# Four edits to the first phase of a hybrid decoder layer on one core: the pace of the decode sample's scores, the engine that takes the low parts of x, the engine that scales the norms' identity, and the order inside a head's split

## The chip, the cores and the metric

The program runs on one core of a Trainium2 chip. Its engines each take their own instructions in order and meet through semaphores: TensorE (PE, with its weight loads shown apart as PEld), VectorE (DVE), ScalarE (ACT), GpSimd (POOL) and SyncE (SP, which here issues nearly all DMA transfers). The metric is the device time of one execution in microseconds. Lower is better.

## The reference, cut to what matters

One layer of a decoder: RMSNorm, one wide projection to q, k, v, u and vc, attention in three dilations for a prompt of 2048 positions, the same attention for 8 decode samples of 4 tokens against a cache of 2048 positions, a gMLP gate, an output projection, an MLP and a gated per-layer embedding, each behind a norm.

```python
z = rmsnorm(h, norm_g) @ w_in                       # (2048 + 32 tokens) x 1024 -> 2560
q, k, v, u, vc = jnp.split(z, ...)                  # 512 columns each
q, k = rope_partial(q, pos), rope_partial(k, pos)
# decode sample: keys gathered by stride 1, 4 and 16 from cache_k (2048 rows, 8 x 64)
s = jnp.einsum('bthd,btkhd->bthk', q, kg) * (HEAD_DIM ** -0.5)
p, lse = softmax_stats(s)
o = jnp.einsum('bthk,btkhd->bthd', p, vg)           # values gathered from cache_v
# prompt: the same, banded, for dilations 1, 4, 16; then gMLP: u * (W_s layernorm(vc) + b)
h = h + concat(attn, gmlp) @ w_out
h = h + relu(rmsnorm(h) @ w_up)**2 @ w_down
h = h + sigmoid(rmsnorm(h) @ w_gate) * (p_ple @ w_ple)
y = rmsnorm(h)
```

Everything is fp32.

## The kernel before, in words

**Three products for one.** An fp32 product is made of three matmuls on rounded operands: each operand is split into a high part (a rounding cast) and a low part (the operand less its high part), and PE adds high x high, high x low and low x high into the same PSUM bank. So in phase A each matmul triple (L306 to L308 for column tiles `f`, L310 to L312 for token tiles `t`) reads `xh`, `xl`, `wh` and `wl`.

**Phase A** is the wide projection and takes the first 615 us. It goes over x three times: pass r=0 makes q and k, r=1 makes v (`t` tiles) and u (`f` tiles), r=2 makes vc (`t` tiles). Each pass goes over four groups g of 544, 512, 512 and 512 columns (tokens; the first group holds the 32 sample tokens), and each group over 8 slices of 128 input features. `x_split` (L190 to L215) makes one slice's `xh` by a cast on ACT (L202) and its `xl` by a subtraction on DVE or POOL (L203); ten slices are live at a time. `w_split` makes `wh` on ACT (L173) and `wl` on DVE (L174). `qk_evac` takes q and k out of PSUM on DVE (L325, L328) into a ring of three tiles `qk`, which come free when SP's stores to `q_d` (L344) and `kT` (L346) have landed.

**The order around the change** is written by the program itself: every engine gets its instructions in the order in which the Python code issues them, and the code is driven by `tick`, which is called after each slice of a unit of matmuls. A tick runs the delayed stores, at most one step of the evacuations, and `bg[1]` steps of a background list `bg[0]`: the rate adds up, and a step is taken when the sum passes one. On that list stand, one behind the other, `sample_k`, `sample_v` and the prologue of the attention. `to_tok` puts `sample_k` there, once k of the sample tokens is known.

**sample_k** makes the decode sample's scores: after two small products with the new keys (L616, L617) it loads rows of `cache_k` (L607) and the broadcast q (L612), and then 48 times multiplies 128 x 1024 elements on POOL (L634) and reduces the product on DVE (L637), one step for each. Two products may be waiting for their reduction. Three of its loads and the first q stand together just ahead of the first product; the text calls these loads the burst. **sample_v** follows at its own rate, 32 casts on ACT (L727) and low parts alternately on DVE and POOL (L728).

**rstd** makes the reciprocal root of a mean square for a group of tokens, four times in phase A and fourteen times in the last phase: PE sums (L97), ACT copies (L104), POOL raises to the power -1/2 (L105), DVE makes a diagonal matrix from the identity (L111; L114 for the 32 sample tokens), PE multiplies it with ones, which spreads it over all partitions (L118, L121), ACT copies that out (L127, L129).

**split_head** makes the operands of a head for the attention in eight steps: ACT casts q and k (L819, L820), POOL subtracts (L811, L813), and `load_piece` (L798) lets SP fetch a later piece. It runs in the prologue for the first head, still inside pass r=2, and between the units of attention for the others. `perm_piece` (L843, ACT) reorders q for the dilations.

**The end of phase A.** The last group's vc tiles go through a Gelu on ACT (L499, tiles `vg`), a layer norm on DVE (L506 to L517, tile `vn`), the spatial product on PE (L531) and the gate on DVE (L544), and when that list is empty the attention begins with its scores on PE (L947), exponentials on ACT (L968) and turns on PE (L976).

Of the kernel before, what the change touches and what calls it, by code (L numbers as in the profile page):

```python
# [8 lines left out]
F32 = mybir.dt.float32  # L9
F32R = mybir.dt.float32r  # L10
AF = mybir.ActivationFunctionType
ALU = mybir.AluOpType
AX = mybir.AxisListType

P = 128
# [5 lines left out]
NS = DB * DS  # L21
# [26 lines left out]
def build(tc, A, stop=9):  # L48
    nc = tc.nc
    V, S, G, T = nc.vector, nc.scalar, nc.gpsimd, nc.tensor  # L50
# [10 lines left out]
    with stack:  # L61
# [4 lines left out]
        ident = cp.tile([P, P], F32, name="ident")  # L66
# [25 lines left out]
        def rstd(ps, nm, ssum, tt, rt, out, tmp, near=1, far=2, sums=None):  # L92
            i0 = int(tt[0][1] < P)
            n = len(tt)
            p = ps.tile([P, 512], F32, tag="sm", name="rc" + nm, bufs=2)
            for i, (o, m) in enumerate(tt):
                T.matmul(p[:m, i:i + 1], ssum[:, o:o + m], ones[:, 0:1], start=True, stop=True)  # L97
            for _ in range(near):
                yield
            t2 = tmp(0)  # L100
            if i0:
                S.copy(t2[:NS, 0:1], p[:NS, 0:1])
                G.tensor_tensor(rt[:NS, 0:1], t2[:NS, 0:1], half[:NS, 0:1], op=ALU.pow)
            S.copy(t2[:, i0:n], p[:, i0:n])  # L104
            G.tensor_tensor(rt[:, i0:n], t2[:, i0:n], half[:, i0:n], op=ALU.pow)  # L105
            for _ in range(far):
                yield
            w = P * (n - i0)
            dg, ds = tmp(1)
            dgv = dg[:, :w].rearrange("p (a b) -> p a b", b=P)  # L110
            V.tensor_mul(dgv, ident.unsqueeze(1).to_broadcast([P, n - i0, P]),  # L111
                         rt[:, i0:n].unsqueeze(2).to_broadcast([P, n - i0, P]))
            if i0:
                V.tensor_scalar(ds, ident[:NS, :NS], rt[:NS, 0:1], None, op0=ALU.mult)  # L114
            for _ in range(near):
                yield
            p = ps.tile([P, 512], F32, tag="sm", name="rb" + nm, bufs=2)
            T.matmul(p[:, :w], one1, dg[:, :w], start=True, stop=True)  # L118
            if i0:
                p2 = ps.tile([P, 512], F32, tag="sm", name="rs" + nm, bufs=2)  # L120
                T.matmul(p2[:, :NS], one1[:NS, :], ds, start=True, stop=True)  # L121
            for _ in range(near):
                yield
            o0 = tt[i0][0]
            if sums is not None:
                sums.append(p[:, :w])
            S.copy(out[:, o0:o0 + w], p[:, :w])  # L127
            if i0:
                S.copy(out[:, 0:NS], p2[:, :NS])  # L129


        def phase_a(sa, ape, prologue):
# [8 lines left out]
            ktok = kp.tile([P, AW], F32, name="ktok")  # L141
# [50 lines left out]
            def x_split():  # L192
                if x_pos[1] == len(x_items):
                    return
                r, g, k = x_items[x_pos[1]]
                n = GROUPS[g][1]
                x_load(x_pos[1] + 1)
                x_pos[2] = clock[0]
                raw = x_raw.pop((r, g, k))
                h = kp.tile([P, GM], F32R, tag="xh", name=f"xh{r}{g}_{k}", bufs=XB)[:, :n]  # L200
                l = kp.tile([P, GM], F32R, tag="xl", name=f"xl{r}{g}_{k}", bufs=XB)[:, :n]
                S.copy(h, raw)  # L202
                (G if r == 2 or (r == 0 and g == 0) else V).tensor_sub(l, raw, h.bitcast(F32))  # L203
                if r == 0:
                    if k == 0:
                        ss[g] = xw.tile([P, GM], F32, tag="ssum", name=f"ss{g}")[:, :n]
                    sq = xw.tile([P, GM], F32, tag="sq", name=f"sq{g}_{k}")[:, :n]
                    S.activation(sq, raw, AF.Square)
                    if k == 0:
                        V.tensor_scalar(ss[g], sq, 8 * EPS, None, op0=ALU.add)  # L210
                    else:
                        V.tensor_add(ss[g], ss[g], sq)
                X[r, g, k] = (h, l)
                x_pos[1] += 1
# [134 lines left out]
            def to_tok(sf, dst, nm):  # L349
# [6 lines left out]
                if nm == "q":  # L356
                    after(2, lambda: nc.sync.dma_start(qs_d, dst))
                else:
                    bg[0].append(sample_k(sb, ktok[:NS], sT, snew))
                    bg[1] = 0.36  # L360


            sb = {t: ape.tile([P, SEQ], F32, tag=t, name="s" + t) for t in ("kl0", "q10", "kh0", "qd2")}
# [212 lines left out]
            return [sb[t].rearrange("p (h j f) -> p h j f", h=2, j=2)[:, x] for t in names for x in range(2)]  # L576


        def sample_k(sb, ktok, sT, snew):
            qbs = halves(sb, ["kl0"])  # L580
            prods = halves(sb, ["q10", "kh0"])
            kts = halves(sb, ["r0", "r1", "qd2"])
# [37 lines left out]
            for t in range(3):  # L620
                load(t)
            load_q(0)
            yield
            load_q(1)
            for t, (b, jj, d) in enumerate(items):
                if len(prs) == 2:
# [175 lines left out]
        def split_head(x):  # L802
# [3 lines left out]
            q1 = atp[hh].tile([P, SEQ], F32R, tag=f"q1{hh}", name=f"q1_{a}_{hh}")  # L806
            kh = atp[hh].tile([P, SEQ], F32R, tag=f"kh{hh}", name=f"kh_{a}_{hh}")
            head[x] = (q1, kh, kl)
            for j in range(9):
                if j:  # L810
                    G.tensor_sub(timed(q1[ot, c]), q[me].rearrange("p (n r a) -> p n r a", r=16, a=8),  # L811
                                 timed(q1[me, c].bitcast(F32)))
                    G.tensor_sub(kl[:, c], k, kh[:, c].bitcast(F32))  # L813
                if j % 2 == 0 and (j or x == 1):
                    load_piece()
                if j < 8:
                    c = slice(256 * j, 256 * j + 256)
                    k, q = (place(4 * x + j // 2)[y][:, 256 * (j % 2):256 * (j % 2) + 256] for y in range(2))
# [995 lines left out]
```

## Time and profile before

| | |
|---|---|
| median of 3 runs | 2939.37 us (2938.58 to 2942.21) |
| the profiled execution's own time | 2937.39 us |
| its span on the core | 2935.6 us |
| PE busy | 2804.6 us, 96% |
| DVE, ACT, POOL busy | 1566.5, 1277.3, 1228.1 us |
| mean granted TensorE clock | 0.973 of full speed |

The span is the time from the first instruction to the last, and 1.8 us lie around it. In a row of the trace the first numbers are the start and the length in us, then follow the engine, the line of the kernel, the operation, output and inputs and the tile's shape; a bracket at the end says how long the engine had been idle before, and which instruction or transfer released it. Engine times overlap, so a busy sum is no time of the kernel; what counts is where PE stands idle.

### The profile page before, as it was taken

How to read it: one execution, taken by the hardware profiler on the slowest of the kernel's cores; microseconds unless marked ns; L12 is line 12 of the kernel's file. 1: busy time of each engine (PE TensorE's matmuls, PEld its weight loads, DVE VectorE, ACT ScalarE, POOL GpSimd, SP SyncE). 2: the span in 40 equal slices, each digit the busy share in tenths (PEclk: the TensorE clock that was granted, in tenths of full speed). 3: DMA queues.
4: the chain of work that ended last, by engine and by line, in shares of the span. 5: the costliest groups of instructions: out<-in, count | busy, mean ns of one | idle time of the engine just before them, and what ended most of it. 6: DMA issues, size and time to landing. Idle time of an engine off the chain costs nothing.

```text
span 2935.6 us, 42217 instructions
## 1 busy us (share of the span) xinstructions
PE 2804.6 (96%) x15712; PEld 2406.1 (82%) x15712; DVE 1566.5 (53%) x3001; ACT 1277.3 (44%) x2293; POOL 1228.1 (42%) x867
## 2 busy tenths in 40 slices
PE   8998998979899898899999999999999999999998
PEld 8776875669888798799999798888888888888887
DVE  6487447655544457754445544546535356535347
ACT  4122253347778674433334333334433434433342
POOL 2255335545668574533223333334333333433332
PEclk9998999979999999899999999999999999999999
DMA  6458766455765765222222242422233423333232
GB/s 188 142 190 286 244 210 221 142 150 176 229 218 160 242 190 187 76 94 87 87 91 85 77 136 93 169 92 99 82 127 114 145 93 101 101 113 122 94 108 71
DMA packets 218478, 413.34 MB, mean 141 GB/s; under 512 B 19552, under 2 KB 87680, under 8 KB 218272
## 3 DMA queue, kind: packets, MB, share of 16 engines
q1 hardware_dynamic: 215584, 406.45, 42.9%
q10 hardware_dynamic: 2688, 4.20, 0.4%
q8 instruction: 124, 2.03, 0.3%
q14 instruction: 82, 0.67, 0.1%
HBM read 342.61 MB, written 67.96 MB: 140 GB/s over the span
## 4 chain that ended last, share of the span: by engine, by line
PE 57%; DVE 2%; ACT 1%; issue 1%; POOL 0%; POOLq 0%; ACTq 0%
PE u L1445 8%; PE u L1443 8%; PE u L1444 8%; PE d L1443 8%; PE d L1444 8%; PE d L1445 8%; PE g L1445 2%; PE g L1444 2%; PE g L1443 2%; DVE ss L1367 1%; PE b L1445 1%; PE b L1443 1%; PE b L1444 1%; DVE zf L1407 0%; ACT sq L1362 0%
## 5 line engine op out<-in xcount | busy, mean ns | idle before, releaser
L1288 POOL TENSOR_TENSOR w<-wraw,w 128x1024 fp32r<-128x1024 f32 x228 | 558.9, 2454 | 993.8 <-ACT w L1287 955.6
L1287 ACT CAST w<-wraw 128x1024 fp32r<-128x1024 f32 x304 | 316.4, 1045 | 368.6 <-PE d L1444 259.8
L1443 PE MATMUL d<-ring,w 128*128 128x512 f32 (+2 forms) x1312 | 458.2, 349 | 0.9 <-ACT ring L1479 0.9
L1493 DVE TENSOR_TENSOR acc<-acc,d 128x512 f32<-128x512 f32 (+2 forms) x640 | 361.0, 578 | 180.9 <-PE d L1445 180.0
L1443 PE MATMUL u<-zh,w 128*128 128x512 f32 (+1 forms) x1280 | 454.0, 355 | 3.0 <-ACT sq L1362 1.8
L1444 PE MATMUL d<-ring,w 128*128 128x512 f32 (+2 forms) x1312 | 455.3, 347 | 0.3 <-DVE ring L1480 0.3
L1445 PE MATMUL d<-ring,w 128*128 128x512 f32 (+2 forms) x1312 | 455.3, 347 | 0.0
L1445 PE MATMUL u<-zh,w 128*128 128x512 f32 (+1 forms) x1280 | 452.1, 353 | 0.0
L1444 PE MATMUL u<-zl,w 128*128 128x512 f32 (+1 forms) x1280 | 449.8, 351 | 2.2 <-POOL zl L1411 1.3
L1480 DVE TENSOR_TENSOR ring<-r,ring 128x512 fp32r<-128x512 f32 (+1 forms) x160 | 112.4, 703 | 514.8 <-ACT ring L1479 514.8
L1443 PEld LDWEIGHTS d<-ring,w 128*128 128x128 f32 x1312 | 248.0, 189 | 32.8 <-ACT ring L1479 1.1
L1445 PEld LDWEIGHTS d<-ring,w 128*128 128x128 f32 x1312 | 247.3, 188 | 33.1
L1444 PEld LDWEIGHTS d<-ring,w 128*128 128x128 f32 x1312 | 247.7, 189 | 31.2 <-DVE ring L1480 0.5
L1444 PEld LDWEIGHTS u<-zl,w 128*128 128x128 f32 x1280 | 242.3, 189 | 37.4 <-issue 1.7
L1443 PEld LDWEIGHTS u<-zh,w 128*128 128x128 f32 x1280 | 241.6, 189 | 37.1 <-ACT sq L1362 2.0
L1445 PEld LDWEIGHTS u<-zh,w 128*128 128x128 f32 x1280 | 241.8, 189 | 32.7
L1477 ACT ACTIVATE r<-u 128x512 f32<-128x512 f32 (+1 forms) x160 | 82.6, 516 | 290.2 <-PE u L1445 290.2
L1136 POOL TENSOR_TENSOR fl<-fr,fh 128x512 fp32r<-128x512 f32 (+1 forms) x120 | 128.5, 1076 | 134.4 <-ACT fh L1135 112.6
L306 PE MATMUL f<-xh,wh 128*128 128x512 f32 (+1 forms) x480 | 174.8, 364 | 8.5 <-ACT wh L173 5.6
L307 PE MATMUL f<-xl,wh 128*128 128x512 f32 (+1 forms) x480 | 172.3, 359 | 7.5 <-DVE xl L203 7.5
L958 DVE CUSTOM_DVE_ANT_0 sm<-s,mask 128x256 f32<-128x256 f32 (+1 forms) x384 | 122.3, 363 | 103.4 <-ACT pe L968 34.1
L308 PE MATMUL f<-xh,wl 128*128 128x512 f32 (+1 forms) x480 | 172.7, 360 | 0.4 <-DVE wl L174 0.4
(279 smaller groups left out, 5708.5 us busy)
## 6 DMA issues: line engine op xcount, KB each, us to landing
wraw<-w_up SPq DMA_DIRECT2D x128, 512.0 KB
wraw<-w_down SPq DMA_DIRECT2D x128, 512.0 KB
xr<-xT SPq DMA_DIRECT2D x72, 256.0 KB
sr<-cache_v SPq DMA_DIRECT2D x32, 512.0 KB
wraw<-w_gate SPq DMA_DIRECT2D x32, 512.0 KB
fr<-g_d SPq DMA_DIRECT2D x24, 512.0 KB
wr<-w_in SPq DMA_DIRECT2D x40, 256.0 KB
o_d<-stg SPq DMA_DIRECT2D x32, 264.0 KB
```

What stands on the lines that cost most here:

```text
L306: T.matmul(p, wh[:, k, ws], h[:, o:o + w], start=st, stop=False)
L307: T.matmul(p, wh[:, k, ws], l[:, o:o + w], start=False, stop=False)
L308: T.matmul(p, wl[:, k, ws], h[:, o:o + w], start=False, stop=sp)
L958: V.tensor_tensor_reduce(sm[:, c], sp[:, c], mask[:, 256 * d + (256 - P * nk if d < 2 else 0):256 * d + (256 if d < 2 else P)], scale=1.0, ...
L1136: G.tensor_sub(l, raw, h.bitcast(F32))
L1287: S.copy(w[:, 0], raw)
L1288: (V if t % 4 == 3 else G).tensor_sub(w[:, 1], raw, w[:, 0].bitcast(F32))
L1443: T.matmul(p, wh, zh, start=(x == 0), stop=False)
L1444: T.matmul(p, wh, zl, start=False, stop=False)
L1445: T.matmul(p, wl, zh, start=False, stop=(x == n - 1))
L1480: V.tensor_sub(hl[:, c], r, hh[:, c].bitcast(F32))
L1493: V.tensor_add(acc[g][:, d, c], acc[g][:, d, c], p)
```

## The change

Four edits. `to_tok` hands `sample_k` the rate setter `pace` and starts it at 0.8 steps per tick, and `sample_k` sets 0.38 when it has issued its first loads; before, the rate was 0.36 throughout. `x_split` gives POOL the low parts of pass r=1 as well, so DVE keeps those of r=0, groups 1 to 3, alone. `rstd` makes its diagonal on ACT, with one copy scaled by a per-partition number for each 128 columns, in place of one multiplication on DVE. `split_head` takes ten steps, and the loads stand at odd steps ahead of POOL's subtractions.

```diff
@@ rstd
-            V.tensor_mul(dgv, ident.unsqueeze(1).to_broadcast([P, n - i0, P]),
-                         rt[:, i0:n].unsqueeze(2).to_broadcast([P, n - i0, P]))
+            for a in range(n - i0):
+                S.activation(dgv[:, a, :], ident, AF.Copy, scale=rt[:, i0 + a:i0 + a + 1])
             if i0:
-                V.tensor_scalar(ds, ident[:NS, :NS], rt[:NS, 0:1], None, op0=ALU.mult)
+                S.activation(ds, ident[:NS, :NS], AF.Copy, scale=rt[:NS, 0:1])
@@ x_split
-                (G if r == 2 or (r == 0 and g == 0) else V).tensor_sub(l, raw, h.bitcast(F32))
+                (G if r or g == 0 else V).tensor_sub(l, raw, h.bitcast(F32))
@@ to_tok
-                    bg[0].append(sample_k(sb, ktok[:NS], sT, snew))
-                    bg[1] = 0.36
+                    bg[0].append(sample_k(sb, ktok[:NS], sT, snew, pace))
+                    bg[1] = 0.8
@@ sample_k
-        def sample_k(sb, ktok, sT, snew):
+        def sample_k(sb, ktok, sT, snew, pace):
...
             load_q(0)
-            yield
+            yield from pace(0.38)
             load_q(1)
@@ split_head
-            for j in range(9):
-                if j:
+            for j in range(10):
+                if j % 2 and (j > 1 or x == 1):
+                    load_piece()
+                if 0 < j < 9:
                     G.tensor_sub(timed(q1[ot, c]), q[me].rearrange("p (n r a) -> p n r a", r=16, a=8),
                                  timed(q1[me, c].bitcast(F32)))
                     G.tensor_sub(kl[:, c], k, kh[:, c].bitcast(F32))
-                if j % 2 == 0 and (j or x == 1):
-                    load_piece()
```

What this does to the engines' orders is shown at three places. First, SP in pass r=0, from the load of the sample's q (`skl`, L591) on; `sr` and `sqd` are the tiles for rows of cache_k, `xr` slices of x, `qk` tiles of q and k. Before, right behind that load:

```order
L188 DMA xr_4_1004<-xT 128x512
L344 DMA q_d<-qk_0_2_994 128x512
L344 DMA q_d<-qk_0_3_1002 128x512
L188 DMA xr_5_1033<-xT 128x512
L188 DMA xr_6_1076<-xT 128x512
L188 DMA xr_7_1096<-xT 128x512
L188 DMA xr_0_1113<-xT 128x512
L607 DMA sr_113<-cache_k 128x512
L607 DMA sr_113<-cache_k 128x1024
L607 DMA sr_114<-cache_k 128x1024
L612 DMA skl_109<-qs_d 128x1024
L344 DMA q_d<-qk_0_0_948 128x512
```

After, right behind the same load:

```order
L607 DMA sr_113<-cache_k 128x512
L607 DMA sr_113<-cache_k 128x1024
L607 DMA sr_114<-cache_k 128x1024
L612 DMA skl_109<-qs_d 128x1024 x2
L607 DMA sqd_112<-cache_k 128x1024
L188 DMA xr_4_1022<-xT 128x512
L344 DMA q_d<-qk_0_2_1010 128x512
L344 DMA q_d<-qk_0_3_1020 128x512
L607 DMA sqd_112<-cache_k 128x1024
L188 DMA xr_5_1054<-xT 128x512
```

The burst has moved ahead of four slices of x and two stores, and away from the store of `qk_0_0`, the tile that it stood right in front of.

Second, the border of passes r=0 and r=1. On DVE before, from the first low part of pass r=1 (`xl_0`, 544 columns) on:

```order
L203 TENSOR_TENSOR xl_0_1711<-xr_0_1476,xh_0_1710 128x544
L325 SCALAR_TENSOR_TENSOR qk_0_2_1714<-f_0_2_0_1603,rstd_b 128x512
L174 SCALAR_TENSOR_TENSOR wl_1688<-wr_1_510,gains,wh_1687 128x512
L325 SCALAR_TENSOR_TENSOR qk_0_3_1726<-f_0_3_0_1604,rstd_b 128x512
L637 TENSOR_REDUCE sT_107<-sq_110 128x16
L174 SCALAR_TENSOR_TENSOR wl_1688<-wr_2_1689,gains,wh_1687 128x512
L203 TENSOR_TENSOR xl_1_1751<-xr_1_1493,xh_1_1750 128x544
L174 SCALAR_TENSOR_TENSOR wl_1688<-wr_3_1716,gains,wh_1687 128x512
L637 TENSOR_REDUCE sT_107<-sq_110 128x16
L203 TENSOR_TENSOR xl_2_1785<-xr_2_1510,xh_2_1784 128x544
```

And on POOL after, from the same low part on:

```order
L203 TENSOR_TENSOR xl_0_1745<-xr_0_1504,xh_0_1744 128x544
L634 TENSOR_TENSOR sq_110<-sr_114,skl_109 128x1024
L203 TENSOR_TENSOR xl_1_1785<-xr_1_1521,xh_1_1784 128x544
L634 TENSOR_TENSOR skh_111<-sr_113,skl_109 128x1024
L203 TENSOR_TENSOR xl_2_1820<-xr_2_1541,xh_2_1819 128x544
L203 TENSOR_TENSOR xl_3_1837<-xr_3_1549,xh_3_1836 128x544
L634 TENSOR_TENSOR skh_111<-sqd_112,skl_109 128x1024
L203 TENSOR_TENSOR xl_4_1854<-xr_4_1762,xh_4_1853 128x544
L203 TENSOR_TENSOR xl_5_1873<-xr_5_1795,xh_5_1872 128x544
L203 TENSOR_TENSOR xl_6_1887<-xr_6_1842,xh_6_1886 128x544
L634 TENSOR_TENSOR sq_110<-sqd_112,skl_109 128x1024
L203 TENSOR_TENSOR xl_7_1908<-xr_7_1860,xh_7_1907 128x544
```

The low parts have left the queue of evacuations, weight parts and reductions on DVE, and stand among four of sample_k's products on POOL.

Third, ACT at the end of phase A, the last two Gelus of vc (`vg_256`, `vg_384`) and the store of the last gate. Before:

```order
L819 CAST q_0_0_4719<-stage_4591 64x2x16x8
L820 CAST kh_0_4720<-stage_4591 128x256
L843 CAST qd_4916<-q_0_0_4719 128x512
L499 ACTIVATE vg_256_4925<-t_4_256_4803,rstd_t 128x512
L843 CAST qd_4916<-q_0_0_4719 128x512 x2
L499 ACTIVATE vg_384_4948<-t_4_384_4877,rstd_t 128x512
L546 DMA g_d<-gt_384_4981 128x4x128
```

After:

```order
L843 CAST qd_4742<-q_0_0_4399 128x512 x2
L499 ACTIVATE vg_0_4854<-t_4_0_4750,rstd_t 128x512
L499 ACTIVATE vg_128_4856<-t_4_128_4751,rstd_t 128x512
L499 ACTIVATE vg_256_4939<-t_4_256_4846,rstd_t 128x512
L499 ACTIVATE vg_384_4960<-t_4_384_4898,rstd_t 128x512
L546 DMA g_d<-gt_384_4993 128x4x128
```

The first head's casts and its three reorderings have all moved ahead of the last group's Gelus, and nothing stands between the last two of these.

## Rows read from the trace of the kernel before

**Rows 1.** Windows by stage: bounds and length, busy per engine, PEclk, DMA share, GB/s.

```profile
0.00:615.00 615.00, 569.44 (x2784) 444.06 (x2784) 390.96 (x559) 202.91 (x387) 261.05 (x149) 0.96 0.61 198
615.00:655.00 40.00, 24.76 (x119) 21.57 (x119) 15.48 (x64) 24.18 (x49) 13.28 (x24) 0.56 0.65 183
1200.00:2935.60 1735.60, 1712.81 (x9261) 1483.45 (x9259) 861.66 (x1282) 670.21 (x1036) 607.08 (x276) 0.99 0.31 103
```

**Rows 2.** Timeline of PE, 119 to 136 us.

```profile
125.71 0.50 PE L307 MATMUL f<-xl,wh 128*128 128x512 f32 x1 [2.58 <-DVE xl L203]
...
131.25 0.51 PE L307 MATMUL f<-xl,wh 128*128 128x512 f32 x1 [3.87 <-DVE xl L203]
```

**Rows 3.** Timeline of DVE, 108 to 134 us.

```profile
123.36 0.69 DVE L328 TENSOR_TENSOR qk<-f,rstd_b 128x512 f32<-128x512 f32 x1 [7.98 <-DMA q_d<-qk]
125.58 2.86 DVE L212 TENSOR_TENSOR ss<-ss,sq 128x512 f32<-128x512 f32 x1
128.37 2.83 DVE L203 TENSOR_TENSOR xl<-xr,xh 128x512 fp32r<-128x512 f32 x1
```

**Rows 4.** Windows around the two stalls of phase A, and a stretch between them.

```profile
130.00:140.00 10.00, 8.75 (x28) 7.28 (x29) 7.12 (x8) 0.16 (x1) 4.76 (x4) 0.66 0.72 237
220.00:245.00 25.00, 15.36 (x44) 8.47 (x45) 23.35 (x24) 6.35 (x10) 10.56 (x4) 0.73 0.77 253
140.00:200.00 60.00, 59.00 (x256) 47.02 (x255) 50.96 (x48) 17.46 (x30) 39.12 (x17) 1.00 0.70 246
```

**Rows 5.** Groups by line on PE, 219.9 to 240.8 us: busy, mean ns, idle before.

```profile
L312 PE MATMUL t<-wl,xh 128*32 128x512 f32 (+1 forms) x11 | 5.5, 504 | 2.1 <-DVE wl L174 2.1
L311 PE MATMUL t<-wh,xl 128*32 128x512 f32 (+1 forms) x11 | 5.5, 502 | 7.6 <-DVE xl L203 7.6
```

**Rows 6.** Groups by line and shape, whole span: busy, mean ns, idle before.

```profile
L634 POOL TENSOR_TENSOR skh<-sr,skl 128x1024 f32<-128x1024 f32 x16 | 40.0, 2505 | 68.3 <-DMA q_d<-qk 41.1 <-DVE sT L637 14.6 <-DMA wr<-w_in 6.7
L203 POOL TENSOR_TENSOR xl<-xr,xh 128x512 fp32r<-128x512 f32 x24 | 35.5, 1486 | 27.0 <-ACT xh L202 27.0
L203 DVE TENSOR_TENSOR xl<-xr,xh 128x512 fp32r<-128x512 f32 x48 | 40.5, 848 | 39.3 <-ACT xh L202 39.0
L203 POOL TENSOR_TENSOR xl<-xr,xh 128x544 fp32r<-128x544 f32 x16 | 26.0, 1631 | 18.8 <-ACT xh L202 18.4 <-DMA xr<-xT 0.4
```

**Rows 7.** Timeline of DVE: the first low part of pass r=1.

```profile
205.28 2.55 DVE L203 TENSOR_TENSOR xl<-xr,xh 128x544 fp32r<-128x544 f32 x1
```

**Rows 8.** Timeline of PE: the first matmul that reads it.

```profile
218.38 0.40 PE L311 MATMUL t<-wh,xl 128*32 128x512 f32 x1
```

**Rows 9.** Timeline of PE, end of phase A and first scores.

```profile
614.75 0.39 PE L312 MATMUL t<-wl,xh 128*128 128x512 f32 x1
621.71 1.97 PE L531 MATMUL sp<-wsT,vn 128*64 128x128 f32 x16 [6.57 <-DVE vn L517]
...
627.28 0.48 PE L947 MATMUL s<-kh,qd 128*128 128x128 f32 x1
```

**Rows 10.** Timeline of ACT, 600 to 641 us.

```profile
617.09 0.68 ACT L499 ACTIVATE vg<-t,rstd_t 128x512 f32<-128x512 f32 x1
...
619.57 0.69 ACT L499 ACTIVATE vg<-t,rstd_t 128x512 f32<-128x512 f32 x1
...
636.33 1.28 ACT L968 ACT_TABLE_LOAD   x1
637.62 1.28 ACT L968 ACTIVATE pe<-sm,stg 128x128 f32<-128x128 f32 x4
```

**Rows 11.** Timeline of PE, the two waits for a norm's diagonal.

```profile
1191.26 2.04 PE L118 MATMUL rb<-dg,one 128*128 128x512 f32 x2 [7.47 <-DVE dgs L114]
...
2864.31 0.70 PE L118 MATMUL rb<-dg,one 128*128 128x256 f32 x2 [1.25 <-DVE dg L111]
```

**Rows 12.** Timeline of DVE, then of ACT, at 1183 to 1193 us.

```profile
1186.00 5.12 DVE L111 TENSOR_TENSOR dg<-ident,rt 128x512 f32<-128x512 f32 x1
...
1186.00 0.63 ACT L1362 ACTIVATE sq<-acc 128x512 f32<-128x512 f32 x1 [0.76 <-DVE ss L1367]
```

## What the change does to the time: the prediction

> **What bounds the kernel now.** I read the windows by stage first, because the share of busy time is an average. From 1200 us on PE is busy 1712.81 of 1735.60 us at 0.99 of the clock, so nothing that the other engines do there can give back more than a few us. Phase A has 45.6 us of PE idle in 615 (615.00 less 569.44), and the 40 us in which it passes into attention have 15.2 us of idle at 0.56 of the clock [rows 1]. So I went to PE's timeline in phase A for its longest waits, then to the timelines of the engines they name, and to the groups by line for the prices.
>
> Two places stand out. At 125 and 131 us PE waits 2.58 and 3.87 us for `xl` from DVE [rows 2]. DVE is not slow there: it had stood 7.98 us before an evacuation (L328) whose `qk` tile was still being stored to `q_d`, and when it got going, its two-input operations, 0.69 us otherwise, took up to 2.86 us [rows 3]. In program order that store stands right behind the burst of `cache_k` loads (front, first place). At 220 to 241 us, the border of passes r=0 and r=1, PE waits 7.6 us for `xl` and 2.1 us for `wl`, both from DVE [rows 5], which is busy 23.35 of the 25 us [rows 4].
>
> **The change part by part.** The sum is made against the profiled execution's own 2937.39 us; the median shown lies 1.98 us above it, and I add that at the end.
>
> *A, the burst.* The loads move ahead of four slices of x and two stores. The store of `qk_0_0` then no longer queues behind them, and the first product comes in group 1. At stake are 6.45 us of waits [rows 2] and what the clock lost after them: from 130 to 140 us it was granted at 0.66 (between its levels of 1.2 and 2.4 GHz) with PE busy 8.75 us [rows 4], which is 8.75 x 0.34 = 3.0 us. What it will look like, the stretch from 140 to 200 us tells: products run there already (POOL busy 39.12 of 60 us), the same operations of pass r=0 are on DVE, and PE idles 1.00 us [rows 4]. I take -6.5: the waits less 1 us, and a third of the clock's loss. Bounds: -9.4 (all of it) and -2 (the tile is waited for elsewhere in the group).
>
> *B, the border.* The eight low parts of group 0 leave DVE. On POOL each takes 1.63 us and stands among four products of 2.5 us (front, second place; the prices [rows 6]): 8 x 1.63 + 4 x 2.5 = 23.0 us. The first was possible at 205.28 [rows 7], a product may be running (2.5 us), so the last is ready at about 230.8. PE reads the first at 218.38 [rows 8] and goes through a slice in six matmuls of 59.00 / 256 = 0.230 us [rows 4], so it wants the last at 218.4 + 7 x 1.38 = 228.0: 2.8 us late in place of 9.7. DVE, rid of 1.2 to 2.9 us pieces, is then the later one with its `wl`, some 1 to 2 us more. I take -5 and let the clock's loss stand. Bounds: -13.8 (all 9.7 us, and 15.36 x 0.27 = 4.1 us of clock [rows 4]) and +2.5 (one more product ahead of the last low part).
>
> *C, the rest of pass r=1.* POOL's program from the first low part of group 0 to the last product holds 22 products, 8 low parts of 544 and 8 of 512 columns: 22 x 2.5 + 8 x 1.63 + 8 x 1.49 = 80 us. Its products also wait for DVE's reductions, 14.6 us in the 16 of one form [rows 6], 0.9 each, so 20 us: 100 us. PE takes 5 + 4 token tiles of 24 matmuls and as much as 4.25 + 4 column tiles of them in the two groups, 414 x 0.230 = 95 us, and the low parts have a head start of 218.4 - 205.3 = 13.1 us [rows 7, 8]. So POOL falls about 5 us behind and eats less than half of the head start. I take +2 for a slice that meets a product, bounds 0 and +6.
>
> The Trainium skill speaks against this edit: GPSIMD Engine Reference, section 4.1, sends two-input elementwise work to VectorE, since GpSimd is about two times slower at it. This trace agrees nearly, 1486 against 848 ns for 128 x 512 [rows 6], a ratio of 1.75 with DVE's contended pieces in its mean. By the page's two, the eight low parts of group 1 would take 8 x 1.70 in place of 8 x 1.49 us, and POOL would be 7 us behind and not 5, which leaves the term as it is.
>
> *D, sample_v and the first head's split move earlier.* They follow sample_k, which ends about one group sooner, so their POOL and ACT work and their transfers lie in other places of passes r=1 and r=2, and `load_piece` stands ahead of the subtractions. The work is the same and PE covers most of it; I take 0, bounds -3 and +6 (two waits as long as those of [rows 2], less the clock).
>
> One side effect is in ACT's order: the sample's exponentials now fall between the Gelus of u, so two more activation tables are loaded (8 against 6). A load is 1.28 us [rows 10]. ACT is busy 202.91 of 615 us [rows 1] and no matmul soon after reads these Gelus, so I take 0, at most +2.6. The Trainium skill, ScalarE: Activation LUTs, section What ACT_TABLE_LOAD costs, gives about 2.7 us with the drain for each; the row here is half of that, and by the page the bound would be +5.4.
>
> *E, the end of phase A.* The last matmul of vc starts at 614.75, but its Gelu at 619.57, because ACT works off the first head's casts and reorderings in between [rows 9, 10]. After, nothing stands there. From the end of the earlier Gelu (617.77) to its spatial product (621.71) the layer norm takes 3.94 us. So: last matmul done 615.15, Gelu done about 615.9, spatial product 619.8, and after its 1.97 us [rows 9] the scores at 621.8 in place of 627.28. The gate, its store and the first exponential at 637.62 [rows 10] follow by the same amount. I take -5.5; bounds -6.5 and -3 (the layer norms of the last two tiles on DVE one behind the other).
>
> *F, the norms.* At 1191.26 PE has waited 7.47 us for the diagonal [rows 11]; DVE had it under way from 1186.00 for 5.12 us [rows 12]. ACT is free at 1186.63 [rows 12]. Four activations of 128 x 128 take 1.28 us there [rows 10], the small one some 0.2, so PE can go at about 1188.2: -3. Of the wait of 1.25 us at 2864.31 [rows 11] I take 1 off. Where DVE had been fast (the first group's norm, the very last one) four small operations are longer than one, by 0.4 each as I assume from the 1.28: +0.8 together. The other norms are made while PE has matmuls to do. Sum -3, bounds -5 and +1 (a cast of the MLP's weights, queued behind the copies on ACT, comes late).
>
> Sum: -6.5 - 5 + 2 + 0 - 5.5 - 3 = -18. 2937.39 - 18 = 2919.4, and with 1.98 **2921 us**.
>
> **The rivals.** *First, the waits only move.* Another `qk` store holds DVE instead, since all stores still share one queue with the cache loads, and at the border `wl` is late by as much as `xl` was. Then A and B are 0, and 2937.39 - 6.5 + 1.98 = 2933. For it: at 123.36 DVE waits for a DMA, not for POOL, so the transfer could be slow by itself [rows 3]. Against it: the stretch from 140 to 200 us, where loads and stores share the queue and PE idles 1 us [rows 4].
>
> *Second, POOL becomes the bound of pass r=1, and the kernel slower.* A low part waits behind products, a product behind its reduction on DVE, and that behind evacuations which wait for PE. With 80 us of work in 95 + 13 us, PE is reached when a product waits over 28 / 22 = 1.3 us on average; the row has 0.9 [rows 6]. At 2 us POOL is 80 + 44 - 108 = 16 us late, the clock falls as it did at 220 us and costs some 4 more, and B's 5 are gone: 25 on top of 2921 is 2946.
>
> *Third, the earlier prologue collides in pass r=2.* The first head's pieces stand in SP's queue ahead of slices of x and wait for POOL, whose subtractions now meet low parts of the same pass. Three waits like the two of [rows 2], with their clock, are 12 us: 2933. Nothing in the trace rules it out, but the end of phase A gains from the same shift, and that is counted.
>
> **How the numbers follow.** The forecast has 0.62, with its own range of 2908 to 2932 from the bounds of A, B and E; the first rival 0.18, the second 0.10, the third 0.10. A difference under 0.2%, 5.9 us, is what a measurement of this kernel can hardly tell from none, so faster means below 2933.5 and slower above 2945.2. The forecast lies below but for 0.01; of the first and third rival a little over half does; the second is slower by half and more. Faster 0.62 + 0.15 = 0.77, slower 0.08, the rest 0.15 the same. The range of 2906 to 2938 reaches over the first and the third rival and leaves out the second and the ends.
>
> **What would show it right or wrong.** A: no wait for `xl` over 1 us at 115 to 135 us, and the first product below 100 us. B: at the border waits of some 4 us in sum, named POOL `xl` or DVE `wl`. C: no wait for POOL's `xl` over 3 us later in pass r=1. E: scores begin 5 to 6 us nearer to the last vc matmul, the two last Gelus one behind the other. F: the wait before L118 near 1188 us on the old scale is about 4.5 us and names ACT. The prediction is wrong if POOL's `xl` in pass r=1 holds PE for over 15 us in sum, or if pass r=2 shows waits that were not there.

## The result and the profile after

The changed kernel takes 2914.84 us in the median of 4 runs (2914.68 to 2915.15) against 2940.79 us for the kernel before (2938.58 to 2944.29, 4 runs): a ratio of 0.9911, interval 0.9894 to 0.9928, or 26 us. The profiled spans are 2913.3 and 2935.6 us, 22.3 us apart; this is the difference that the stages below add up to. The kernel before varies by several us between executions, which the medians take in and one profile does not.

The windows by stage, as in [rows 1], with bounds moved to the same places of the program (phase A now ends near 603 us):

```profile
0.00:605.00 605.00, 564.30 (x2784) 440.71 (x2784) 365.31 (x527) 214.45 (x411) 300.58 (x184) 0.97 0.63 203
605.00:650.00 45.00, 34.31 (x195) 31.12 (x196) 19.27 (x80) 29.17 (x62) 19.80 (x29) 0.62 0.69 197
1190.00:2913.30 1723.30, 1702.55 (x9220) 1474.20 (x9220) 831.57 (x1256) 679.68 (x1075) 601.66 (x273) 1.00 0.31 103
```

PE's idle time in phase A is 40.7 us where it was 45.6 (1.5 of the 40.7 lie behind the last matmul, which the window before does not have), with the same 2784 matmuls; the rest of the gain there is PE's busy time, 564.3 us against 569.4, at 0.97 of the clock in place of 0.96. Around the two places of [rows 4], 130 to 140 us and 25 us at the border of the passes:

```profile
130.00:140.00 10.00, 10.00 (x43) 7.78 (x42) 4.46 (x6) 3.39 (x8) 10.00 (x6) 1.00 0.99 382
210.00:235.00 25.00, 23.62 (x102) 16.72 (x101) 18.82 (x18) 7.83 (x12) 23.15 (x11) 1.00 0.97 320
```

Both run at the full clock, and PE is idle 1.4 us in the second, where it was idle 9.6. PE's timeline shows the waits that are new, changed or left at the places of the prediction, to be read beside [rows 2], [rows 5] and [rows 9]:

```profile
173.03 0.50 PE L307 MATMUL f<-xl,wh 128*128 128x512 f32 x1 [2.35 <-DVE xl L203]
...
213.58 0.40 PE L311 MATMUL t<-wh,xl 128*32 128x512 f32 x1
...
223.51 0.42 PE L312 MATMUL t<-wl,xh 128*32 128x512 f32 x1 [1.22 <-DVE wl L174]
...
224.72 0.42 PE L311 MATMUL t<-wh,xl 128*32 128x512 f32 x1
...
248.89 0.59 PE L306 MATMUL f<-xh,wh 128*128 128x272 f32 x1 [4.67 <-ACT vo L423]
...
458.71 1.05 PE L739 MATMUL so<-sel,skh 64*128 64x4 f32 x8 [3.38 <-DVE skh L734]
...
603.09 0.39 PE L312 MATMUL t<-wl,xh 128*128 128x512 f32 x1
605.88 1.09 PE L531 MATMUL sp<-wsT,vn 128*64 128x128 f32 x16 [2.40 <-DVE vn L517]
609.61 1.97 PE L531 MATMUL sp<-wsT,vn 128*64 128x128 f32 x16 [2.64 <-DVE vn L517]
611.51 0.48 PE L947 MATMUL s<-kh,qd 128*128 128x128 f32 x1
```

The waits of 2.58 and 3.87 us are gone, one in the next group has grown from 1.00 to 2.35 us, the border has 1.22 us left, and the one for `vo` (a v tile, taken out of PSUM by ACT) is 4.67 us where it was 2.00. At 213.58 and 224.72 us stand the first and the last reading of a low part in the border's first pair of token tiles. From the last vc matmul to the scores it is 8.4 us where it was 12.5.

Where POOL stands at the border, by its timeline (the answer to [rows 7]):

```profile
195.13 1.82 POOL L203 TENSOR_TENSOR xl<-xr,xh 128x544 fp32r<-128x544 f32 x1
196.92 2.84 POOL L634 TENSOR_TENSOR sq<-sr,skl 128x1024 f32<-128x1024 f32 x1
199.72 1.82 POOL L203 TENSOR_TENSOR xl<-xr,xh 128x544 fp32r<-128x544 f32 x1
...
209.92 1.37 POOL L203 TENSOR_TENSOR xl<-xr,xh 128x544 fp32r<-128x544 f32 x1 [3.63 <-ACT xh L202]
...
222.86 1.81 POOL L203 TENSOR_TENSOR xl<-xr,xh 128x544 fp32r<-128x544 f32 x1
```

The first norm of the last phase on ACT, and the wait on PE that goes with it, as in [rows 12] and [rows 11]:

```profile
1170.17 1.26 ACT L112 ACTIVATE dg<-ident,rt 128x128 f32<-128x128 f32 x4
1171.34 0.30 ACT L114 ACTIVATE dgs<-ident,rt 32x32 f32<-32x32 f32 x1
...
1171.49 2.08 PE L118 MATMUL rb<-dg,one 128*128 128x512 f32 x2 [3.89 <-ACT dg L112]
```

Setting the two timelines of PE side by side at the same instruction gives the stages. The columns are the time of that instruction in the two profiles and how the gap grew since the line above; the instructions are the sums of the norms (L97) of groups 1 to 3, the first matmul of v, the first of u, the last of vc, the first scores, and two spreadings of a norm (L118) in the last phase.

```text
                     before    after     gap    grown by
sums, group 1         79.38    80.69    +1.31    +1.31
sums, group 2        133.27   126.81    -6.46    -7.77
sums, group 3        183.03   178.22    -4.81    +1.65
first of v           218.15   213.35    -4.80    +0.01
first of u           261.11   242.93   -18.18   -13.38
last of vc           614.75   603.09   -11.66    +6.52
first scores         627.28   611.51   -15.77    -4.11
first norm, last ph. 1191.26  1171.49  -19.77    -4.00
a later norm         1661.80  1640.78  -21.02    -1.25
end of the span      2935.60  2913.30  -22.30    -1.28
```

(The gap between the first of u and the last of vc is compared at its ends only, since sample_v's matmuls have moved in between. The first line holds nothing of the edits that these runs can tell: `xl_alone`, which leaves that stretch as it was, is 1.85 us late there.)

### The profile page after: what moved, and what is told of

Its sections match the earlier page's. It is cut to its first block, busy times and chain, and to the rows that moved or that the text cites. A ratio compares the mean times of both kernels' runs of the same rounds, so it can differ in the third digit from the quotient of the medians.

```text
span 2913.3 us, 42298 instructions
## 1 busy us (share of the span) xinstructions
PE 2798.0 (96%) x15712; PEld 2399.5 (82%) x15712; DVE 1515.2 (52%) x2947; ACT 1299.9 (45%) x2363; POOL 1265.0 (43%) x899
## 4 chain that ended last, share of the span: by engine, by line
PE 57%; DVE 2%; ACT 1%; issue 0%; POOL 0%; POOLq 0%; ACTq 0%; DVEq 0%
PE u L1445 8%; PE u L1443 8%; PE u L1444 8%; PE d L1443 8%; PE d L1444 8%; PE d L1445 8%; PE g L1445 2%; PE g L1444 2%; PE g L1443 2%; DVE ss L1367 1%; PE b L1443 1%; PE b L1445 1%; PE b L1444 1%; DVE zf L1407 0%; ACT sq L1362 0%
```

## The experiments

Times are medians, set against the kernel before, timed beside them on the same chip. The changed kernel was not timed again beside them, and the medians of the kernel before differ by up to 2.8 us between these groups of runs (2937.96 to 2940.79); so a difference to the changed kernel under some 3 us is not resolved.

**The four edits one by one.** `pace_alone` is the kernel before with the hunks of the diff in `to_tok` and `sample_k`:

```diff
-                    bg[1] = 0.36
+                    bg[1] = 0.8
...
-            yield
+            yield from pace(0.38)
```

> The kernel before with the new pace alone (0.8 up to the first product, 0.38 from there). My theory: this edit carries A and E by itself. The waits of 2.58 and 3.87 us at 125 to 131 us go, with their clock (-7 to -8 us to the third group's sums, as in the changed kernel), and the last Gelus of vc stand one behind the other (-4 us between the last vc matmul and the scores). The border of passes r=0 and r=1 keeps its waits of about 9.7 us, since the low parts are still on DVE. Time -9 to -14 us against before. Rival: the loss at 125 us only went because the low parts are off DVE later and the border had room; then the pace alone moves the products into DVE's busiest stretch, new waits appear there, and the time is within 5 us of before.

Measured: 2925.10 against 2939.67 us, ratio 0.9945 (0.9933 to 0.9958). The places at 125 us and at the end of phase A came as my theory had it (the gap is -7.5 us at the sums of group 2, and -4.1 us from the last vc matmul to the scores). But 3.3 us come back in group 3, another 3.1 us behind it (38.2 us from the sums of group 3 to the first of v in place of 35.1, PE without idle time, at 0.91 of the clock in place of 1.00), and the border did not keep its waits:

```profile
225.37 0.41 PE L311 MATMUL t<-wh,xl 128*32 128x512 f32 x1 [0.93 <-DVE xl L203]
231.79 0.42 PE L312 MATMUL t<-wl,xh 128*32 128x512 f32 x1 [2.34 <-DVE wl L174]
```

With a third of 0.43 us between them, and the low parts still on VectorE, PE waits 3.7 us there in place of 9.7, and the stretch from the first of v to the first of u is 32.3 us where it was 43.0. So VectorE is not too full for the border; something else had made it late.

`xl_alone`:

```diff
-                (G if r == 2 or (r == 0 and g == 0) else V).tensor_sub(l, raw, h.bitcast(F32))
+                (G if r or g == 0 else V).tensor_sub(l, raw, h.bitcast(F32))
```

> The kernel before with the low parts of pass r=1 on GpSimd alone. My theory: the border loses its waits (-13 us there with the clock, as in the changed kernel) and later waits in pass r=1 take some back; the stall at 125 us stays. Time -8 to -13 us. Rival: without the earlier products GpSimd has 27 products left at the border in place of 22 and falls behind, low parts come late in groups 1 and 2, and the time is -5 to +5 us.

Measured: 2932.37 us, ratio 0.9971 (0.9960 to 0.9983), -7.3 us. The border is 34.2 us long, 8.7 less, and 4.7 us of waits for `wl` are left on PE; no wait names a low part on GpSimd in pass r=1. That is a little less than my theory had, for it had put all 13 us of the border down to this edit; the rival is out.

`diag_alone` (the hunk in `rstd`):

> The kernel before with the norms' diagonal on ScalarE alone. My theory: the wait before the first norm of the last phase falls from 7.5 to about 3.9 us, two short waits late in the program change by a few tenths, and the time is -3 to -5 us. Rival: the last phase as a whole gains (the changed kernel is 2.5 us shorter from that norm to the end), because VectorE is rid of nine to fourteen slow operations there; then -6 us or more.

Measured: 2934.51 us, ratio 0.9979 (0.9970 to 0.9989), -5.2 us, just over the theory's end. The wait at the first norm is 3.89 us, as it should be, but the sums of group 3 come 2.7 us later, of which 1.2 are still there at the scores. That the norms of phase A do this is not shown: 1.5 of the 2.7 us stand already at the sums of group 1, where `xl_alone`, with the old diagonal, is late too. The rival, a gain in the whole last phase, is not borne out: from the first norm to the end it is 1742.0 us, and 1741.6 to 1742.7 us in the other single edits with the old diagonal.

`split_alone` (the hunk in `split_head`):

> The kernel before with the new order inside a head's split alone. My theory: the loads move past subtractions in a stretch in which TensorE is covered; -2 to +1 us. Rival: the earlier loads are what lets the first head's casts finish before the last Gelus, and this edit carries the gain at the end of phase A: -4 us or more.

Measured: 2934.53 us, ratio 0.9982 (0.9973 to 0.9991), -5.1 us by the medians and -1.5 by the profiled spans (2934.1 against 2935.6). Neither theory is borne out. From the last vc matmul to the scores it takes 10.1 us in place of 12.5, so a part of the rival's gain is there; but the last vc matmul comes 3.7 us later, and the scores start 1.3 us later than before. No stage of the profile shows a gain of 4 us, and why the medians do stays open.

**One number in place of the edits.** In the kernel before, VectorE had waited 7.98 us for the store of a q tile [rows 3], and the same kind of wait stands in its timeline at the border:

```profile
215.13 0.69 DVE L325 SCALAR_TENSOR_TENSOR qk<-f,rstd_b 128x512 f32<-128x512 f32 x1 [6.04 <-DMA q_d<-qk]
```

These stores are asked for 12 ticks after the tile is made, and SyncE takes its issues in order, so each stands behind loads which wait for free tiles. `store_early` is the kernel before with

```diff
-                    after(12 if g and m < 2 else 2, lambda: nc.sync.dma_start(q_d[m, :, c0 + s0 - NS:c0 + n - NS], o_[:, s0:]))
+                    after(2, lambda: nc.sync.dma_start(q_d[m, :, c0 + s0 - NS:c0 + n - NS], o_[:, s0:]))
```

> The kernel before with one number changed: the stores of the first two q tiles of groups 1 to 3 are asked for 2 ticks after the tile is made, in place of 12, so on SyncE they stand ahead of the burst and of the loads behind it. Theory: both waits of phase A, the one at 125 us and the one at the border of passes r=0 and r=1, begin with VectorE waiting for a q tile whose store stands late in SyncE's queue (7.98 us at 115 us, 6.04 us at 209 us). Then this number alone takes most of both away: -8 to -18 us, with neither the pace nor the low parts moved. Rival for the border: VectorE is simply too full there (23.4 of 25 us busy), so the border keeps over 6 us of waits for xl and only the first place gains: -4 to -9 us. Rival for both: the stores are slow as transfers, the wait stays: within 3 us of before.

Measured: 2919.75 against 2937.96 us, ratio 0.9938 (0.9924 to 0.9952), -18.2 us from a single number. SyncE's timeline has the stores, and VectorE's has the only wait for a q tile that is left between 100 and 240 us:

```profile
94.65 0.93 SPq L344 DMA_DIRECT2D q_d<-qk  x2
96.78 1.45 SPq L344 DMA_DIRECT2D q_d<-qk  x2
...
151.15 0.69 DVE L325 SCALAR_TENSOR_TENSOR qk<-f,rstd_b 128x512 f32<-128x512 f32 x1 [0.36 <-DMA q_d<-qk]
```

and PE's groups by line from 209 to 244 us show the border's waits:

```profile
L311 PE MATMUL t<-wh,xl 128*128 128x512 f32 (+1 forms) x40 | 16.4, 411 | 2.6 <-DVE xl L203 2.6
L312 PE MATMUL t<-wl,xh 128*128 128x512 f32 (+1 forms) x40 | 16.4, 410 | 2.1 <-DVE wl L174 2.1
```

The first store is issued at 94.65 us; before, it stood behind the burst until 113.99:

```profile
112.10 1.37 SPq L607 DMA_DIRECT2D sr<-cache_k  x3
113.52 0.43 SPq L612 DMA_DIRECT2D skl<-qs_d  x1
113.99 0.43 SPq L344 DMA_DIRECT2D q_d<-qk  x1
```

The place at 125 us is gone (-7.5 us at the sums of group 2) and the border keeps 4.7 of 9.7 us (-8.2 us by its length of 34.8). So the late store alone made the first wait, and about half of the second; the rival for both is out, and that for the border (over 6 us of waits for `xl`) too. What was late about it is less its issue than its landing. VectorE began to stand at 115.38, when the store had been issued, and was let go at 123.36, 9.4 us after the issue (8.3 us in `xl_alone`, which keeps the burst in its place); the store at 96.49 had let VectorE go after 2.9 us. In the changed kernel the same store is issued hardly sooner, and VectorE takes the tile at 119.92 without a wait:

```profile
111.26 1.45 SPq L607 DMA_DIRECT2D sr<-cache_k  x1
113.00 0.33 SPq L188 DMA_DIRECT2D xr<-xT  x1
113.38 0.42 SPq L344 DMA_DIRECT2D q_d<-qk  x1
...
119.92 0.68 DVE L328 TENSOR_TENSOR qk<-f,rstd_b 128x512 f32<-128x512 f32 x1
```

One load of `cache_k` is issued in the 2.2 us ahead of it there, in place of three and one of q. VectorE also gets to the tile 4.5 us later than before, having a reduction and a lengthened addition to do, which covers a part.

**What the low parts' move is worth beyond the border.** `pool_g0` is the changed kernel with

```diff
-                (G if r or g == 0 else V).tensor_sub(l, raw, h.bitcast(F32))
+                (G if r == 2 or g == 0 else V).tensor_sub(l, raw, h.bitcast(F32))
```

> The changed kernel, but of pass r=1 only group 0 has its low parts on GpSimd; groups 1 to 3 are back on VectorE. Theory: all that the move to GpSimd earns lies at the border, and the rest of it is neutral, since in the changed kernel no wait in pass r=1 names a low part: +-2 us against the changed kernel, -24 us against before. Rival (term C of the prediction): the low parts of groups 1 to 3 on GpSimd cost 2 us or more through the products and through sample_v, and the time is 2 to 6 us below the changed kernel.

Measured: 2915.54 against 2937.96 us, ratio 0.9921 (0.9908 to 0.9934), within a microsecond of the changed kernel by the medians, 3.5 us by the two differences to the kernel before. The 24 low parts of groups 1 to 3 cost and earn nothing on GpSimd that these runs resolve; the rival, a time below the changed kernel's, is out. The wait for `vo` is there too, 3.93 us, so it does not come from them.

**The changed kernel without one edit.** `no_pace` has the old rate, `no_diag` the old diagonal.

> The changed kernel without the pace: low parts, diagonal and split as changed, the rate 0.36 throughout. Theory: the pace and the low parts each take away the border's wait by themselves, so their gains overlap; what the pace adds on top of the other three is the place at 125 us (-7 us, of which 3 come back in group 3) and the end of phase A (-4 us). So this one is 7 to 11 us slower than the changed kernel, -14 to -18 us against before. Rival: the gains add up, and without the pace 14 us are missing: -9 to -11 us against before.

> The changed kernel with the diagonal back on VectorE. Theory (term F, -3 in the prediction): the first norm of the last phase gives 3.5 us, the short ones a little, and phase A loses 1 to 2 us at its first norm, so without the edit the kernel is 2 to 5 us slower than the changed one, 2917 to 2920. Rival: with the q stores early the edit brought next to nothing in the median, because what the norm gives the earlier stages take back; then the time is within 1.5 us of the changed kernel.

Measured: `no_pace` 2922.17 against 2937.96 us, ratio 0.9941 (0.9929 to 0.9954), 7 us above the changed kernel, as the theory of overlapping gains has it, and the rival is out. Its profile is not as the theory has it: the border takes 36.4 us in place of 29.6, with 4.7 us of waits for `wl`, and 5.7 of these 6.8 us come back between the first of u and the last of vc. `no_diag` 2921.94 against 2938.80 us, ratio 0.9944 (0.9930 to 0.9957), 7 us above it as well, more than the theory's 5, and the rival is out. By the profiles 2.7 us of these stand at the scores (2.1 already at the sums of group 3; what makes them is not shown) and 3.6 at the first norm of the last phase, where PE waits 7.32 us again.

**Towards a faster version.** After the change the one wait over 1 us in groups 1 to 3 of pass r=0 is that at 173 us. `g3_pool` moves eight more low parts, `changed_store` has the early stores in the changed kernel, `g3_and_store` both, and `store_and_diag` is the kernel before with the early stores and the new diagonal only.

```diff
-                (G if r or g == 0 else V).tensor_sub(l, raw, h.bitcast(F32))
+                (G if r or g in (0, 3) else V).tensor_sub(l, raw, h.bitcast(F32))
```

> The changed kernel with the low parts of pass r=0, group 3 on GpSimd as well. Theory: of the waits in the changed kernel's pass r=0 only one of 2.35 us for VectorE's xl is left, at 173 us, where VectorE's two-input operations are stretched by the products; GpSimd has room for eight more pieces of 1.5 us between its products, and the time falls by 2 to 4 us against the changed kernel. Rival: a low part behind a product which waits for its reduction comes later than VectorE's, and the time is 0 to 4 us above the changed kernel.

> The changed kernel with the q stores asked for after 2 ticks. Theory: the wait of 2.35 us at 173 us follows one of 2.38 us of VectorE for a q tile; with the store early it shrinks, and the time is 2 to 5 us below the changed kernel, near the one with group 3 on GpSimd. Rival: that wait comes from the products beside VectorE alone, and the time stays within 1.5 us of the changed kernel.

> The changed kernel with the low parts of pass r=0, group 3 on GpSimd, and with the q stores asked for after 2 ticks. Theory: in the kernel with group 3 on GpSimd no wait of pass r=0 over 1 us is left, so the stores have nothing more to give: within 2 us of that kernel, about -28 us against before. Rival: VectorE still waits 2 to 3 us for q tiles in groups 1 to 3, and with the stores early 3 us or more come on top: -31 us against before.

> The kernel before with the q stores early and the diagonal on ScalarE; no pace, no low parts moved, no split. Theory: the two act in different places and add up, -18 and -4.5 us against before: 2915 to 2917, about the changed kernel's time with two of its four edits left out. Rival: the diagonal's four pieces on ScalarE delay the casts of pass r=0 (its sums came 1 to 2 us later with the diagonal alone), and the time is 2919 or more.

Measured: `g3_pool` 2909.99 against 2937.96 us, ratio 0.9903 (0.9889 to 0.9916), 5 us under the changed kernel by the medians (2 us by the differences to the kernel before); the sums of group 3 come 11.0 us before those of the kernel before, in the changed kernel 4.8. `changed_store` 2913.97 against 2938.63 us, ratio 0.9915 (0.9902 to 0.9929), 1 us under the changed kernel. Its wait at 173 us shrinks to 0.67, with another of 1.47 before the group's sums, and these come 3.1 us sooner than in the changed kernel; but from there to the first of v it takes 38.25 us in place of 35.13, PE without idle time, at 0.91 of the clock in place of 1.00. So the time is the rival's, but not its reason: the store has its part in the wait, and the clock behind it takes the gain back. `g3_and_store` 2907.71 us, ratio 0.9894 (0.9881 to 0.9908), the fastest here, between the two theories. `store_and_diag` 2919.35 us, ratio 0.9934 (0.9920 to 0.9947), the rival's time. In its profile the norm's wait has shrunk all the same (7.30 to 3.88 us); it is 0.5 us ahead of `store_early` at the first of u, 2.0 behind at the start of pass r=2 and 4.5 behind at the last vc matmul. The windows of the two from 425 to 475 us, `store_early` first:

```profile
425.00:475.00 50.00, 44.05 (x211) 28.75 (x210) 32.11 (x74) 18.97 (x45) 22.39 (x15) 0.97 0.63 211
```

```profile
425.00:475.00 50.00, 45.76 (x198) 30.18 (x196) 28.49 (x66) 17.21 (x40) 20.72 (x15) 0.86 0.66 221
```

PE is busy longer and does 13 matmuls less: that execution had 0.86 of the clock there. There is no norm in this stretch, and at the sums of group 3 it was 0.7 us ahead, so the rival's reason, later casts in pass r=0, is not what the profile shows; why the clock was lower there stays open.

## Why the prediction came out as it did

The time lies inside the range, 6 us under the forecast of 2921, and the sign of each large term is right. That the sum is this near is luck in part, since errors of opposite sign cancel; by the table of stages:

- **A, -6.5 forecast, -7.8 measured, and +1.65 given back in group 3.** The step is right and shown: the burst ahead of the store made it, since moving the store alone does the same. In the changed kernel it worked through how soon the store landed, not through when it was issued (113.38 us and 113.99). The first rival, that the wait only moves, is right for a quarter of it.
- **B, -5 forecast, -13.4 measured.** The step that failed is "the first was possible at 205.28": that row [rows 7] was VectorE's own lateness, not the moment when the slice was there. The cast that makes the slice's high part ends at 197.28 in the kernel before, 8.0 us ahead of it (row below). On GpSimd the first low part ran at 195.13 and PE read it at 213.58, 18.4 us later and not 13.1; the last ended at 224.67 and was read at 224.72, with 1.22 us lost to `wl` in between. The chain on GpSimd was mis-sized as well: 29.5 us and not 23.0, since it stood 5.5 us waiting for casts, which the sum left out. PE never waited for a low part, but with 0.05 us to spare: the wait for `wl` covered the last one. Of the 8.4 us that the term was too small, 3.3 are waits (8.3 us of idle time gone) and 5.1 are the clock's loss, which I had let stand: PE is busy 28.20 us in that stage where it was 33.25, at 1.00 of the clock in place of 0.84. I had also named the wrong reason, a VectorE busy 23.35 of 25 us; `pace_alone` and `store_early` leave the low parts on it and halve the wait. About half of its lateness was the 6.04 us that it had waited for a q store, as in A; the other half, by `xl_alone`, went with the low parts. (The halves are rough, for in `xl_alone` the wait for the q store is 2.58 us too.)
- **C, +2, and D, 0, together +6.5.** No wait for a low part on GpSimd came, and by `pool_g0` this part is worth nothing that can be told; the second rival had no ground. What came in pass r=1 was the wait for `vo`, 2.67 us longer, and in pass r=2 PE's waits over 0.35 us sum to 17.6 us in place of 13.7. The largest new one there is 3.38 us for sample_v (`skh`, L734), whose place the pace has moved: the third rival's direction with another step, at a third of its price. The step that failed is D's "PE covers most of it", put at nothing; new waits in pass r=2 were the prediction's own sign of being wrong. From the first of u to the last of vc `pace_alone` loses 4.4 of the 6.5 us and `split_alone` 3.5, `xl_alone` and `store_early` none; `no_pace`, which has the split too, loses 0.8, so the pace's part is shown and the split's is not.
- **E, -5.5 forecast, -4.1 measured.** The Gelus stand one behind the other as foreseen, and the 1.4 us that are missing are what the bound of -3 names: the two last layer norms follow each other on VectorE, 3.7 us apart, since the gates of the tiles ahead come first. `pace_alone` has the same 2.40 and 2.64 us of waits and the whole 4.1 us, so the pace is enough for it; the split by itself earns 2.4 (`split_alone`, 10.1 us, and `no_pace`, 10.0, in place of 12.5), and the two do not add up.
- **F, -3 forecast, -3.6 at the first norm**, which is the step's own mechanism: ACT makes the diagonal by 1171.6 in five pieces of 1.56 us together. At 2864.31 nothing was gained (1.56 us in place of 1.25). Of the 2.5 us behind the first norm, 1.25 lie before that at 1661.80, a stretch in which the profile of the kernel before is 0.7 to 1.9 us longer than those of all the others, also of kernels with the old diagonal; so they are not shown to be the edit's.

For B, the cast in the kernel before, and the windows from the first of v to the first of u, before and after:

```profile
196.65 0.63 ACT L202 CAST xh<-xr 128x544 fp32r<-128x544 f32 x1
...
218.15:261.11 42.96, 33.25 (x121) 22.45 (x120) 37.88 (x34) 11.72 (x18) 21.91 (x9) 0.84 0.79 259
213.35:242.93 29.58, 28.20 (x122) 20.48 (x121) 24.16 (x22) 10.15 (x16) 24.21 (x12) 1.00 0.94 310
```

For C, ACT's timeline of the changed kernel shows what `vo` waits for, the loads of `w_in` behind `wh`. PE got there 18.2 us sooner, the last of these loads only 15.5; the last two rows are those of the kernel before:

```profile
244.81 0.72 ACT L173 ACTIVATE wh<-wr,gains 128x512 fp32r<-128x512 f32 x1 [3.99 <-DMA wr<-w_in]
247.54 0.72 ACT L173 ACTIVATE wh<-wr,gains 128x512 fp32r<-128x512 f32 x1 [2.01 <-DMA wr<-w_in]
248.17 1.82 ACT L423 ACTIVATE vo<-t,rstd_t 128x512 f32<-128x512 f32 x3
...
263.06 0.72 ACT L173 ACTIVATE wh<-wr,gains 128x512 fp32r<-128x512 f32 x1 [3.79 <-DMA wr<-w_in]
263.69 1.82 ACT L423 ACTIVATE vo<-t,rstd_t 128x512 f32<-128x512 f32 x3
```

And the groups by line of the changed kernel bear on the ratio that the Trainium skill gives in GPSIMD Engine Reference, section 4.1 (about two times): 1382 against 743 ns is 1.86, nearly that. By `pool_g0` it costs nothing that these runs resolve:

```profile
L203 POOL TENSOR_TENSOR xl<-xr,xh 128x512 fp32r<-128x512 f32 x48 | 65.9, 1382 | 43.3 <-ACT xh L202 41.9 <-DMA sqd<-cache_k 1.4
...
L203 DVE TENSOR_TENSOR xl<-xr,xh 128x512 fp32r<-128x512 f32 x24 | 17.8, 743 | 7.2 <-ACT xh L202 7.1
```

So by the spans the sum was 4 us too small (-18 against -22.3): B was 8.4 us too small and what came behind the scores 3.5, while A (-4.8 up to the first of v) was 1.7 too good and C, D and E together 5.9. The other 2 us are the 1.98 that I added for the median of the kernel before; the changed kernel's runs lie within 0.5 us, and its profiled run needed no such correction.

## What to carry to other kernels

When an engine that PE waits for has itself been idle just before, follow that idle time first. Here both large waits named VectorE's low parts, and before both VectorE had waited for a buffer whose store was issued late, or landed late, behind loads in the same DMA queue; asking for that store sooner, one number, takes 18 us off, where the four edits take 26. A row that shows when an operation ran is not evidence of when it could have run: look for its input's time before using it as a head start.

## What the runs showed of the hardware that was not expected

The kernel before spreads over 2933.8 to 2943.3 us in 21 runs, and the changed one over 0.5 us in 4. The pair of windows above, of two kernels, shows that the clock can be 0.97 or 0.86 in the same stage, with PE's waits there alike, 0.6 to 2.0 us each; whether this makes the spread of one kernel is not shown.

A two-input operation on VectorE beside a product on GpSimd does not run at half speed: it stands until the product has ended. In the kernel before all 21 of the lines L174, L203, L212 and L337 to L339 that take over 1.2 us between 60 and 300 us end 0.55 to 0.58 us after a product or low part on GpSimd, whatever their length; in the other profiles it is the same, 0.54 to 0.58 us. These have both inputs in SBUF. L325 and L328, with `f` in PSUM as one input, take 0.67 to 0.69 us in the middle of a product. Two rows of the kernel before:

```profile
236.98 2.76 POOL L634 TENSOR_TENSOR skh<-sr,skl 128x1024 f32<-128x1024 f32 x1 [6.69 <-DMA wr<-w_in]
237.45 2.84 DVE L174 SCALAR_TENSOR_TENSOR wl<-wr,gains,wh 128x512 fp32r<-128x512 f32 x1
```
